# Attention heads by twos with the gates between the pairs, raw float32 weights for the shared expert and the router, and three leading experts with 16 blocks fetched before the sort

## The chip, the cores and the metric

The kernel runs on one core of one Trainium2 chip. The metric is the device time of one execution in microseconds (us); the engines of the core are TensorE (PE, with its weight loads PEld), VectorE (DVE), ScalarE (ACT), GpSimd (POOL) and SyncE (SP), whose queue issues the weight loads here.

## What is computed

Two blocks run one after the other on 256 tokens of 1024 float32 values. Cut to what matters:

```python
# block 1: h = rmsnorm(x); proj = h @ w_in, split into
qa, ka, va, qb, kb, vb, ga, gb = jnp.split(proj, IN_SPLIT_POINTS, axis=-1)
ya = neighbourhood_attention(qa, ka, va, rpb)         # 8 heads of 64, biased and masked scores
qh, kh = axial_rope(rmsnorm(qb, gq)), axial_rope(rmsnorm(kb, gk))
yb = gqa_attention(qh, kh, vb)                        # 8 heads of 64 on 2 key heads
x = x + (sigmoid(ga) * (ya @ w_proj_a) + sigmoid(gb) * (yb @ w_proj_b)) @ w_out
x = x + peer(rmsnorm(x), ...)
# block 2: a token mixer, then the expert layer
scores = sigmoid(xt @ w_router)                       # 64 experts, 8 chosen for each token
routed = sum of gate * (silu(x @ w_gate) * (x @ w_up)) @ w_down over the chosen experts
shared = (silu(xt @ ws_gate) * (xt @ ws_up)) @ ws_down
out = rmsnorm(h + g2 * (routed + shared))
```

## The kernel before, in words

**Weights.** Blocks of 128 x 1024 float32 values (512 KB) come from HBM through SP's queue into rotating buffers. Most products are made from two parts: `split` (L65) lets ACT copy a block to `whi` in the engine's reduced float format and DVE (or POOL, if it is named) subtract to get `wlo`; `mm3` (L78 to L82) then makes three matmuls, high by high, high by low and low by high. A product in plain float32 is one matmul instead, which shows as two records in the trace.

**Block 1** (`block1_mix`). `stationary` (L168) makes one 128-column piece of a projection with the weights in the array, `moving` (L179) makes 512 or 256 columns with the tokens in the array. `qk_block` (L174) makes the q and k of the neighbourhood attention, `moving` its v (`va`), then q (`pq`) and k, v (`pkv`) of the grouped attention. POOL adds the mask to the bias table at once (L246). `attention` (L197) runs one pair of heads: for each head, scores `pS` from its 64 rows (L204), scale and bias on DVE (L211), the maximum (L213, or L216 and L217 without bias), exponentials on ACT (L220), the scaling by the sum (L222, L224), transposes `pT` (L228) and a copy `PT` on ACT (L230); then the value product `pY` with all 128 columns for each head (L235), of which one half of the rows is kept. Between the two attentions stands the rope chain (L268 to L309): squares `sq` (L277), their sums, an inverse root in thirteen small DVE steps (L100 to L110), multiplies by the norms, the rotation (L291 to L299), and the transposes `pqT` (L304) and `pkT` (L308). Sixteen gate blocks `pg` (L316 to L319) stand last in the code; eight of them have their low parts made on POOL; their sigmoids (L321) go four blocks at a time. From here on a list scheduler sets the order on every engine, and it puts the gates' matmuls wherever PE would wait.

**Expert layer** (`moe`). The mixer's output projection, the norm and the shared expert alternate; `gu_block` (L1547) and `shared_up` make the shared expert's first product, L1600 onwards the router. After the router DVE sorts the experts by their number of tokens; `lst` (L1765) holds the sorted list, and SP reads it (L1811) before it can fetch a weight block by rank. The expert of rank r brings six blocks, four `w_gu` and two `w_dn`. The work goes by units of 128 token slots: one rank alone, or 96 + 32, 64 + 64 or four times 32 slots, set by `mixture` (L1445). In one unit's time a PE makes `pgu` (L1559) for it, gathers tokens for later ones (`pga`, L1743), makes the second product `py` (L1578) of the unit before and adds the one before that into the result (`combine`, L1840). The first `STATIC` ranks are units of one rank on tables of their own; as many blocks as fit are fetched before the sort for the experts 0 and onwards. Blocks are used in a fixed order, and each takes the buffer that was used longest ago (`wide_load`, L1407); SP's load waits until PE has used what lay there. The ranks per unit are 1 1 1 2 2 2 4 2 1 2 2 2 1 2 2 4 2 2 2 1 2 2 3 2 2 1, in all 26 units, 50 ranks and 300 blocks, on 25 buffers. Ranks that don't fit run in extra branches (L1940 onwards).

Of the kernel before, what the change touches and what calls it, by code (L numbers as in the profile page):

```python
# [11 lines left out]
F32 = mybir.dt.float32  # L12
# [130 lines left out]
def block1_mix(e, a, x, begin):  # L143
# [22 lines left out]
    qkT = pool.tile([P, 8, T], F32, name="qkT")  # L166

    def stationary(blk, out, eng=None):  # L168
        wh, wl = load_w(e, a["w_in_a"][blk], eng=eng)
# [9 lines left out]
    def moving(blks, width, per):  # L179

        pt = [ps.tile([P, 512], F32, tag="mm", name=uid(e, "pmv"), bufs=e.mm_bufs) for _ in range(2)]
        for i, b in enumerate(blks):
            wh, wl = load_w(e, a["w_in_b"][b])
# [13 lines left out]
    def attention(pair, q_of, k_of, v_of, bias_of, dst):  # L197

        PT = []
        for j in range(2):  # L200
            s = slice(j * 64, (j + 1) * 64)
            pS = ps.tile([P, 2, T], F32, tag="att", name=uid(e, "pS"), bufs=e.att_bufs)
            for i, tt in enumerate((1, 0)):
                nc.tensor.matmul(pS[:, i], q_of(pair)[s, tt * P:(tt + 1) * P], k_of(pair)[s], start=True, stop=True)  # L204
# [41 lines left out]
    nc.gpsimd.tensor_tensor(bias.rearrange("p a b c -> p (a b) c"), bias.rearrange("p a b c -> p (a b) c"),  # L246
                            mask[:, None, :].to_broadcast([P, 48, 64]), op=OP.add)
# [9 lines left out]
    bv = bias.rearrange("p h v c -> p h (v c)")  # L257
    for pair in range(4):
        attention(pair, lambda q: qkT[:, q], lambda q: qkT[:, 4 + q],
                  lambda q, kc: va[:, kc, q * P:(q + 1) * P], lambda h: bv[:, h], yT[0])  # L260

# [18 lines left out]
    for tt, qk in enumerate(qks):  # L280
# [28 lines left out]
        nc.vector.tensor_copy(kT[:, :, tt * P:(tt + 1) * P], p[:, :2])  # L309
    for pair in range(4):  # L310
# [1734 lines left out]
```

## Time and profile before

| what | value |
|---|---|
| time, median of 3 runs | 1756.07 us (1755.73 to 1756.47) |
| profiled execution, its own time | 1763.74 us |
| its span in the trace | 1761.9 us |
| granted TensorE clock over the span | 0.981 |
| PE busy | 1660.2 us (94%) |
| DVE, ACT, POOL busy | 1133.1, 750.5, 190.5 us |
| HBM read | 386.79 MB, 221 GB/s over the span |
| chain that ended last | PE 67%, DVE 18%, DMA 7%, issue 4%, ACT 3% |

The trace is of one execution, whose time is a little over that of the runs; starts and durations are us from the start of its span. An engine's idle time costs something only where the chain runs through it. "Granted clock" is TensorE's clock as a share of full speed.

### The profile page before, as it was taken

What the parts mean: (1) busy time and instruction counts of PE and PEld (TensorE: products, weight loads), DVE (VectorE), ACT (ScalarE), POOL (GpSimd) and SP (SyncE); (2) the same over time, 40 slices, a digit from 0 to 9 for tenths busy, and PEclk for the clock granted to TensorE, in tenths of its full rate; (3) what the DMA queues carried; (4) which work ended last, traced back from release to release, by engine and by line L of the source; (5) the groups of instructions that cost most, each with busy time, mean ns of one, the idle gap of its engine ahead of it and who ended that gap; (6) DMA issues with size and microseconds to landing.
All of it is one profiled execution on the core that took longest, in us unless ns stands there. A gap on an engine that the chain in (4) does not pass through costs nothing.

```text
span 1761.9 us, 29814 instructions
## 1 busy us (share of the span) xinstructions
PE 1660.2 (94%) x11419; PEld 1307.8 (74%) x11419; DVE 1133.1 (64%) x2214; ACT 750.5 (43%) x1224; POOL 190.5 (11%) x95
## 2 busy tenths in 40 slices
PE   6989999899989999999999997987989999999996
PEld 6778888899989999777788776977875444444443
DVE  5675779995989999877777767688673111111112
ACT  3547544444544444444444455655552222222222
POOL 1030001222111222000000003023020000000000
PEclk9999999999999999999999999998999999999999
DMA  6423654556545555587888754532067799999993
GB/s 232 131 84 109 214 163 158 160 158 192 155 126 162 169 171 177 172 283 265 308 283 295 261 165 144 181 118 72 13 238 282 266 392 409 409 402 409 409 409 132
DMA packets 108118, 390.91 MB, mean 222 GB/s; under 512 B 12656, under 2 KB 12944, under 8 KB 107840
## 3 DMA queue, kind: packets, MB, share of 16 engines
q1 hardware_dynamic: 106128, 384.58, 62.7%
q0 software_dynamic: 976, 2.82, 0.5%
q8 instruction: 91, 1.49, 0.3%
q10 hardware_dynamic: 864, 1.53, 0.3%
q14 instruction: 59, 0.48, 0.1%
HBM read 386.79 MB, written 2.10 MB: 221 GB/s over the span
## 4 chain that ended last, share of the span: by engine, by line
PE 67%; DVE 18%; DMA 7%; issue 4%; ACT 3%; POOL 0%; SPq 0%; DVEq 0%; ACTq 0%
PE pgu L1559 11%; PE acc L686 10%; PE py L1578 6%; PE pu L80 5%; PE pu L81 5%; PE pu L82 5%; DVE wlo L67 5%; DMA raw<-in_w_ada 4%; PE pga L1743 3%; PE py L1840 3%; PE pg L632 2%; ACT whi L66 2%; PE pmv L81 1%; PE pmv L82 1%; PE pmv L80 1%
## 5 line engine op out<-in xcount | busy, mean ns | idle before, releaser
L66 ACT ACTIVATE whi<-raw 128x1024 fp32r<-128x1024 f32 x366 | 384.5, 1054 | 307.7 <-PE pu L81 136.7
L67 DVE TENSOR_TENSOR wlo<-raw,whi 128x1024 fp32r<-128x1024 f32 x310 | 383.4, 1239 | 83.1 <-ACT whi L66 82.0
L82 PE MATMUL pu<-pxT,wlo 128*128 128x256 f32 x1024 | 289.7, 283 | 9.2 <-DVE wlo L67 6.7
L80 PE MATMUL pu<-pxT,whi 128*128 128x256 f32 x1024 | 292.3, 285 | 0.8 <-ACT whi L66 0.8
L81 PE MATMUL pu<-pxT,whi 128*128 128x256 f32 x1024 | 288.9, 282 | 0.0
L686 PE MATMUL acc<-whi,hh 128*128 128x512 f32 x1008 | 280.7, 396 | 8.5 <-ACT hh L66 5.8
L686 PEld LDWEIGHTS acc<-whi,hh 128*128 128x128 f32 x1008 | 189.1, 189 | 53.9 <-ACT hh L66 6.8
L67 POOL TENSOR_TENSOR wlo<-raw,whi 128x1024 fp32r<-128x1024 f32 x56 | 149.6, 2675 | 661.9 <-ACT whi L66 607.2
L82 PEld LDWEIGHTS pu<-pxT,wlo 128*128 128x128 f32 x1024 | 195.3, 191 | 11.1 <-DVE wlo L67 8.1
L80 PEld LDWEIGHTS pu<-pxT,whi 128*128 128x128 f32 x1024 | 195.4, 191 | 1.0 <-ACT whi L66 1.0
L81 PEld LDWEIGHTS pu<-pxT,whi 128*128 128x128 f32 x1024 | 195.4, 191 | 0.0
L1559 PE MATMUL pgu<-raw,xg 128*32 128x512 f32 (+2 forms) x1012 | 193.8, 597 | 0.0
L686 PE MATMUL acc<-wlo,hh 128*128 128x512 f32 x504 | 157.5, 393 | 2.8 <-DVE wlo L67 2.8
L66 ACT ACTIVATE hh<-H 128x256 fp32r<-128x256 f32 x126 | 52.6, 417 | 174.6 <-PE acc L686 169.9
L1559 PEld LDWEIGHTS pgu<-raw,xg 128*32 128x32 f32 (+2 forms) x1012 | 55.6, 124 | 92.3 <-issue 82.1
L686 PEld LDWEIGHTS acc<-wlo,hh 128*128 128x128 f32 x504 | 95.0, 189 | 24.3 <-DVE wlo L67 4.2
L67 DVE TENSOR_TENSOR yl<-py,yh 128x512 fp32r<-128x512 f32 x52 | 36.0, 691 | 110.7 <-ACT yh L66 110.6
L1578 PE MATMUL py<-raw,th 128*32 128x512 f32 (+2 forms) x504 | 99.9, 599 | 0.5 <-ACT th L1572 0.5
L1564 DVE SCALAR_TENSOR_TENSOR hh<-hh,sv,pgu 128x256 f32<-128x256 f32 x26 | 12.4, 478 | 124.5 <-ACT hh L1563 124.5
L771 DVE SCALAR_TENSOR_TENSOR ada<-raw,cs,ada 128x1024 f32<-128x1024 f32 x48 | 61.5, 1282 | 40.6 <-DMA raw<-in_w_ada 40.6
L1746 ACT ACTIVATE xg<-pga 128x256 f32<-128x256 f32 x104 | 40.0, 384 | 111.6 <-PE pga L1743 107.6
L1743 PEld LDWEIGHTS pga<-S,hs 128*128 128x128 f32 x416 | 54.5, 188 | 36.8 <-issue 36.1
(567 smaller groups left out, 2919.5 us busy)
## 6 DMA issues: line engine op xcount, KB each, us to landing
raw<-in_w_gu SPq DMA_DIRECT2D x186, 512.0 KB, 9.6
raw<-in_peer_u SPq DMA_DIRECT2D x128, 512.0 KB, 3.6
raw<-in_peer_v SPq DMA_DIRECT2D x128, 512.0 KB, 4.5
raw<-in_w_dn SPq DMA_DIRECT2D x90, 512.0 KB, 10.1
raw<-in_w_ada SPq DMA_DIRECT2D x48, 512.0 KB, 4.8
raw<-in_w_in_a SPq DMA_DIRECT2D x24, 512.0 KB, 3.6
raw<-in_w2a SPq DMA_DIRECT2D x17, 512.0 KB, 4.4
raw<-in_w_out SPq DMA_DIRECT2D x16, 512.0 KB, 3.6
```

The costliest lines, as they stand in the source:

```text
L66: e.nc.scalar.activation(hi, src, AF.Copy)
L67: (eng or e.nc.vector).tensor_sub(lo, src, hi.bitcast(F32))
L80: nc.tensor.matmul(out, lh, rh, start=first, stop=False)
L81: nc.tensor.matmul(out, lh, rl, start=False, stop=False)
L82: nc.tensor.matmul(out, ll, rh, start=False, stop=last)
L686: nc.tensor.matmul(acc[tt][n], h[l][:, s], w[r][:, n * 512:(n + 1) * 512], start=j == order[0] and i == 0, stop=j == order[-1] and i == 2)
L771: nc.vector.scalar_tensor_tensor(mod[n], w, cs[:, c:c + 1], mod[n], op0=OP.mult, op1=OP.add)
L1559: nc.tensor.matmul(pg[t], xx[:, c, t], ws[i][:, k * 512:(k + 1) * 512], start=c == 0, stop=c == NC8 - 1)
L1578: nc.tensor.matmul(py[q][t], th[:, k, t], w[i][:, q * 512:(q + 1) * 512], start=k == 0, stop=last and k == 1)
L1743: nc.tensor.matmul(p[:, :n].rearrange("p u n -> p (u n)"), hs[i][:, tt, q * P:(q + 1) * P], S[:, tt, :n].rearrange("p u n -> p (u n)"), st ...
L1746: nc.scalar.activation(xg[:, q, :n], p[:, :n], AF.Copy)
L1840: nc.tensor.matmul(acc[tt][n], St[:, tt * P:(tt + 1) * P], y[:, n * 512:(n + 1) * 512], start=first and v == 0 and w == 0, stop=v == len(u ...
```

## The change

1. Block 1 loads its weights with `wide_load` and four instead of two pairs of split buffers.
2. `attention` makes the scores of both heads of a pair in turns, and the value product as 64-column halves of one tile, followed by one split of 128 rows instead of two of 64.
3. The mask add becomes four DVE operations of 768 columns, each ahead of the pair that reads it.
4. The projections `pq`, `pkv` and the rope chain come before the neighbourhood attention; each of the eight pairs is followed by two gate blocks; all splits of the gates are on DVE.
5. The shared expert's first product and the router use raw float32 weights and tokens: 16 matmuls instead of 48 and 8 instead of 24.
6. `STATIC` is 3 instead of 2, so 16 instead of 10 blocks are fetched before SP reads the list. `WIDE` and `MID` give other slot widths to the ranks. There are 25 units with the ranks 1 1 1 1 2 2 4 2 2 2 2 2 2 1 4 2 2 2 2 2 2 4 2 2 1, again 50 ranks and 300 blocks, on 27 buffers.

```diff
     qkT = pool.tile([P, 8, T], F32, name="qkT")
+    load = wide_load(e, [(e.stage, e.raw_bufs)], [(e.stage, e.w_bufs), (pool, 2)])
...
+        heads = [slice(j * 64, (j + 1) * 64) for j in range(2)]
+        pSs = [ps.tile([P, 2, T], F32, tag="att", name=uid(e, "pS"), bufs=e.att_bufs) for _ in heads]
+        for i, tt in enumerate((1, 0)):
+            for s, pS in zip(heads, pSs):
+                nc.tensor.matmul(pS[:, i], q_of(pair)[s, tt * P:(tt + 1) * P], k_of(pair)[s], start=True, stop=True)
         PT = []
-        for j in range(2):
-            s = slice(j * 64, (j + 1) * 64)
-            pS = ps.tile([P, 2, T], F32, tag="att", name=uid(e, "pS"), bufs=e.att_bufs)
-            for i, tt in enumerate((1, 0)):
-                nc.tensor.matmul(pS[:, i], q_of(pair)[s, tt * P:(tt + 1) * P], k_of(pair)[s], start=True, stop=True)
+        for j, pS in enumerate(pSs):
...
-        pY = ps.tile([P, 2, T], F32, tag="att", name=uid(e, "pY"), bufs=e.att_bufs)
-        for j in range(2):
-            for kc in range(2):
-                nc.tensor.matmul(pY[:, j], v_of(pair, kc), PT[j][:, kc], start=kc == 0, stop=kc == 1)
-        for j in range(2):
-            s = slice(j * 64, (j + 1) * 64)
-            split(e, dst[0][s, pair], dst[1][s, pair], pY[s, j])
+        pY = ps.tile([P, 512], F32, tag="mm", name=uid(e, "pY"), bufs=e.mm_bufs)[:, :T]
+        for kc in range(2):
+            for s, pt in zip(heads, PT):
+                nc.tensor.matmul(pY[s], v_of(pair, kc)[:, s], pt[:, kc], start=kc == 0, stop=kc == 1)
+        split(e, dst[0][:, pair], dst[1][:, pair], pY)
...
-    nc.gpsimd.tensor_tensor(bias.rearrange("p a b c -> p (a b) c"), bias.rearrange("p a b c -> p (a b) c"),
-                            mask[:, None, :].to_broadcast([P, 48, 64]), op=OP.add)
...
+    def gate(b):
+        p = ps.tile([P, 512], F32, tag="mm", name=uid(e, "pg"), bufs=e.mm_bufs)
+        stationary(8 + b, p[:, :T])
+        nc.scalar.activation(sg[:, b], p[:, :T], AF.Copy)
...
+    def masked(h):
+        if h % 2 == 0:
+            v = bias[:, h:h + 2].rearrange("p a b c -> p (a b) c")
+            nc.vector.tensor_tensor(v, v, mask[:, None, :].to_broadcast([P, 12, 64]), op=OP.add)
+        return bv[:, h]
...
+    for pair in range(4):
+        attention(pair, lambda q: qkT[:, q], lambda q: qkT[:, 4 + q],
+                  lambda q, kc: va[:, kc, q * P:(q + 1) * P], masked, yT[0])
+        for b in (2 * pair, 2 * pair + 1):
+            gate(b)
     for pair in range(4):
         attention(pair, lambda q: qT[:, q], lambda q: kT[:, q // 2],
                   lambda q, kc: vb[:, kc, q // 2].rearrange("p a b -> p (a b)"), None, yT[1])
-
-
-    sg = keep.tile([P, 16, T], F32, name="sg")
-    for b in range(16):
-        p = ps.tile([P, 512], F32, tag="mm", name=uid(e, "pg"), bufs=e.mm_bufs)
-        stationary(8 + b, p[:, :T], nc.gpsimd if b < 8 else None)
-        nc.scalar.activation(sg[:, b], p[:, :T], AF.Copy)
+        for b in (8 + 2 * pair, 9 + 2 * pair):
+            gate(b)
...
-STATIC = 2
-WIDE = 7
-MID = 16
+STATIC = 3
+WIDE = 6
+MID = 14
...
-RAW0 = 4
-RAW1 = 3
+RAW0 = 12
+RAW1 = 5
...
-    def gu_block(pg, xh, xl, b, w):
+    def gu_block(pg, x, b, w):
         for k in range(2):
             c = 2 * b + k
-            s = slice(k * 512, (k + 1) * 512)
-            for j, (l, r) in enumerate(((xh, 0), (xh, 1), (xl, 0))):
-                nc.tensor.matmul(pg, l[:, c], w[r][:, s], start=c == 0 and j == 0, stop=c == NC8 - 1 and j == 2)
+            nc.tensor.matmul(pg, x[:, c], w[:, k * 512:(k + 1) * 512], start=c == 0, stop=c == NC8 - 1)
...
-        mm3(e, p[:, :T], wh[:, c], wl[:, c], hT[0][:, c], hT[1][:, c], c == 0, c == NC8 - 1)
+        nc.tensor.matmul(p[:, :T], wr[:, c], hT[:, c], start=c == 0, stop=c == NC8 - 1)
```

The order that comes of it, at three places. PE, before, at the rope chain: `pqT` and `pkT` are the transposes of the rotated q and k, `pg` are gates.

```order
L82 MATMUL pg_1208<-hT_97,wlo_1212 128x256
L80 MATMUL pg_1208<-hT_97,whi_1211 128x256
L304 MATMUL pqT_884<-ident,qk_841 128x128 x4
L308 MATMUL pkT_890<-ident,kd_880 128x128 x2
L81 MATMUL pg_1208<-hT_98,whi_1211 128x256
L82 MATMUL pg_1208<-hT_97,wlo_1212 128x256
L80 MATMUL pg_1240<-hT_97,whi_1243 128x256
```

PE, after the change, at the same chain; `pmv` is the last projection of k and v, `pS_711` to `pS_826` are the scores of the first two pairs.

```order
L82 MATMUL pmv_572<-whi_605,hT_98 128x256
L205 MATMUL pS_711<-qkT 128x256
L205 MATMUL pS_712<-qkT 128x256
L205 MATMUL pS_711<-qkT 128x256
L205 MATMUL pS_712<-qkT 128x256
L205 MATMUL pS_825<-qkT 128x256 x2
L205 MATMUL pS_826<-qkT 128x256 x2
L298 MATMUL pqT_679<-ident,qk_636 128x128 x4
L302 MATMUL pkT_685<-ident,kd_675 128x128 x2
L298 MATMUL pqT_700<-ident,qk_644 128x128 x4
```

Where gates stood on both sides of the transposes, now only four score products stand between the last projection and the first transpose; the first gate comes after both halves of q and the first pair's probabilities.

ACT, after the change, between the gates of the second pair and the third pair (`sg` are gates, `S_945` and `S_964` the third pair's two heads, `PT` the copy of the transposed probabilities).

```order
L310 ACTIVATE sg<-pg_875 128x256
L66 ACTIVATE whi_1138<-raw_1136 128x1024
L310 ACTIVATE sg<-pg_907 128x256
L331 ACT_TABLE_LOAD
L331 ACTIVATE sg<-sg 128x1024
L223 ACT_TABLE_LOAD
L223 ACTIVATE S_945,sm_947<-S_945,mx_946 128x256 x2
L223 ACTIVATE S_964,sm_966<-S_964,mx_965 128x256 x2
L233 ACTIVATE PT_962<-pT_957 128x512
```

The sigmoid of the first four gates and its two table loads stand between the last of these gates and the third pair's exponentials; before, other gates' copies stood on either side of such a sigmoid.

SP, before, ahead of its first read of the sorted list (`raw` and `ada` are buffers).

```order
L1417 DMA raw_14343<-in_w_gu 128x1024
L1417 DMA raw_14345<-in_w_dn 128x1024
L1417 DMA ada_9413<-in_w_dn 128x1024
L1811 TENSOR_LOAD lst
L1811 ISA x2
```

And after the change:

```order
L1427 DMA raw_14258<-in_w_gu 128x1024
L1427 DMA raw_14260<-in_w_dn 128x1024
L1427 DMA raw_14262<-in_w_dn 128x1024
L1427 DMA raw_14264<-in_w_gu 128x1024
L1427 DMA raw_14266<-in_w_gu 128x1024
L1427 DMA raw_14268<-in_w_gu 128x1024
L1427 DMA raw_14270<-in_w_gu 128x1024
L1427 DMA ada_9400<-in_w_dn 128x1024 x2
L1824 TENSOR_LOAD lst
```

Six more blocks, those of the third leading expert, stand ahead of the read.

## Rows read from the trace of the kernel before

**Rows 1.** Windows: start:end, length, busy of PE, PEld, DVE, ACT, POOL (records), PE clock, DMA share, GB/s

```profile
14.20:54.50 40.30, 36.85 (x243) 34.21 (x242) 22.60 (x22) 12.26 (x12) 6.78 (x1) 0.96 0.58 188
54.50:173.10 118.60, 109.67 (x686) 93.28 (x686) 78.68 (x159) 71.03 (x150) 19.66 (x8) 0.97 0.32 98
...
1430.00:1728.00 298.00, 297.84 (x1997) 132.59 (x1994) 47.81 (x106) 64.18 (x150) 0.00 (x0) 1.00 1.02 408
...
110.00:120.00 10.00, 6.81 (x46) 6.67 (x46) 8.69 (x15) 5.00 (x6) 3.08 (x2) 0.83 0.31 93
```

**Rows 2.** Timeline of POOL and DVE, block 1's start: start, length, engine, line, operation

```profile
16.90 6.78 POOL L246 TENSOR_TENSOR bias<-bias,mask 128x3072 f32<-128x3072 f32 x1 [15.58 <-DMA mask<-in_na_mask]
...
19.38 5.38 DVE L67 TENSOR_TENSOR wlo<-raw,whi 128x1024 fp32r<-128x1024 f32 x1 [0.55 <-ACT whi L66]
```

**Rows 3.** DVE's groups from 44 to 180 us: total busy, mean ns of one

```profile
L67 DVE TENSOR_TENSOR wlo<-raw,whi 128x1024 fp32r<-128x1024 f32 x20 | 24.5, 1224 | 16.8 <-ACT whi L66 16.6
```

**Rows 4.** PE's waits from 14 to 215 us: total us, times, longest

```profile
PE pqT L304 <- DVE qk L299: 4.1, 2, 2.9
PE pqk L82 <- DVE wlo L67: 3.5, 1, 3.5
```

**Rows 5.** Timeline of PE, gate matmuls after the first wait for the rotated q

```profile
113.72 0.41 PE L80 MATMUL pg<-hT,whi 128*128 128x256 f32 x1
113.94 0.41 PE L81 MATMUL pg<-hT,whi 128*128 128x256 f32 x1
...
115.06 0.28 PE L81 MATMUL pg<-hT,whi 128*128 128x256 f32 x1
115.18 0.28 PE L82 MATMUL pg<-hT,wlo 128*128 128x256 f32 x1
```

**Rows 6.** Timeline of PE, scores of two heads, of one head, and value products

```profile
54.43 1.14 PE L204 MATMUL pS<-qkT 64*128 64x256 f32 x8
...
62.44 1.89 PE L235 MATMUL pY<-PT,va 128*128 128x256 f32 x8
...
129.24 1.13 PE L204 MATMUL pS<-kT,qT 64*128 64x256 f32 x4
```

**Rows 7.** The chain that ended last, expert layer: start, length, engine, line, records

```profile
1323.13 5.81 PE pgu L1552 x24
...
1348.27 3.43 PE pgu L1559 x8
...
1380.27 1.88 PE py L1840 x8
...
1385.59 3.57 PE pgu L1559 x32
...
1708.42 1.88 PE py L1840 x8
```

**Rows 8.** Timeline of DVE, the rope chain's first squares and first sum

```profile
90.66 0.81 DVE L277 TENSOR_TENSOR sq<-qk 128x640 f32<-128x640 f32 x1
...
92.72 2.00 DVE L277 TENSOR_TENSOR sq<-qk 128x640 f32<-128x640 f32 x1
...
111.16 0.68 DVE L299 TENSOR_TENSOR qk<-qk,ro 128x512 f32<-128x512 f32 x1
```

**Rows 9.** ACT's groups from 44 to 180 us: total busy, mean ns of one

```profile
L230 ACT ACTIVATE PT<-pT 128x512 f32<-128x512 f32 x16 | 9.5, 600 | 10.0 <-PE pT L228 9.9
...
L220 ACT ACTIVATE S<-pS,mx 128x256 f32<-128x256 f32 x16 | 7.4, 470 | 3.1 <-DVE mx L217 3.1
...
L321 ACT ACTIVATE sg<-sg 128x1024 f32<-128x1024 f32 x4 | 4.2, 1060 | 0.1
...
L321 ACT ACT_TABLE_LOAD x3 | 3.8, 1283 | 0.1
```

**Rows 10.** Windows in the expert phase, columns as in rows 1

```profile
1380.00:1390.00 10.00, 10.00 (x61) 4.67 (x63) 2.53 (x5) 2.48 (x6) 0.00 (x0) 1.00 0.59 179
...
1728.00:1732.00 4.00, 4.00 (x12) 1.82 (x11) 0.28 (x1) 0.38 (x1) 0.00 (x0) 1.00 0.33 131
```

More of the change, by code (lines that the diff above doesn't have):

```diff
@@ L182, in moving @@
         for i, b in enumerate(blks):
-            wh, wl = load_w(e, a["w_in_b"][b])
+            wh, wl = load(a["w_in_b"][b])
             wh, wl = (w.rearrange("p (c n) -> p c n", c=per) for w in (wh, wl))
@@ L1445, in mixture @@
 def mixture():
-    few = iter(range(LIGHT, REST))
+    few = list(range(LIGHT, REST))
+    n = MID - WIDE
     kinds = [[shared((r, P)) for r in range(STATIC, WIDE)],
-             [shared((r, 96), (next(few), 32)) for r in range(WIDE, MID)],
-             [shared((r, 64), (r + 1, 64)) for r in range(MID, LIGHT, 2)]]
-    few = list(few)
-    kinds.append([shared(*((r, 32) for r in few[i:i + 4])) for i in (0, 4)] + [shared((few[8], 32), (few[9], 32), (few[10], 64))])
+             [shared((WIDE + i, 96), (few[i], 32)) for i in range(n)],
+             [shared((r, 64), (r + 1, 64)) for r in range(MID, LIGHT, 2)],
+             [shared(*((r, 32) for r in few[i:i + 4])) for i in range(n, len(few), 4)]]
     at = lambda k, j, n: j / (n - 1) if k == 0 else (j + 0.5) / n
@@ L1474, in moe @@
     mod = m.mod
-    load = wide_load(e, [(early, RAW0), (e.stage, e.raw_bufs)], [(early, 4), (e.stage, e.w_bufs)])
+    load = wide_load(e, [(early, RAW0), (e.stage, e.raw_bufs)], [])
     def add_to(t, p, n, g):
@@ L1503, in moe @@
     square(0, 0)
-    wg = [load(a["ws_gu"][b]) for b in range(2)]
+    wg = [load(a["ws_gu"][b], True) for b in range(2)]
     for i in range(4):
@@ L1512, in moe @@
     add_to(1, po[1], 0, mod[2])
-    wg.append(load(a["ws_gu"][2]))
-    wr = load(a["w_router"], eng=nc.gpsimd)
+    wg.append(load(a["ws_gu"][2], True))
+    wr = load(a["w_router"], True)
     square(1, 0)
@@ L1522, in moe @@
     hs = [pool.tile([P, 2, D], F32R, name=f"hs{i}") for i in range(2)]
-    hT = pool.tile([P, 2, NC8, T], F32R, tag="ehT", name="ehT")
-    hT = [hT[:, i] for i in range(2)]
+    hT = pool.tile([P, NC8, T], F32, tag="ehT", name="ehT")
     load.raw.extend([(pool, RAW1, "raw")] * RAW1)
@@ L1528, in moe, with turn_in @@
         normed(0, r, n)
-    lows = [turned(e, h[0], 4 * n, 0, *hT) for n in range(2)]
+    def turn_in(tt, n):
+        p = ps.tile([P, 4, P], F32, tag="tr", name=uid(e, "ptr"), bufs=e.tr_bufs)
+        for k in range(4):
+            nc.tensor.transpose(p[:, k], h[tt][:, (4 * n + k) * P:(4 * n + k + 1) * P], e.ident)
+        nc.scalar.activation(hT[:, 4 * n:4 * n + 4, tt * P:(tt + 1) * P], p, AF.Copy)
+    for n in range(2):
+        turn_in(0, n)
     add_to(1, m.po[1], 1, mod[2])
     square(1, 1)
-    for f in lows:
-        f()
     r = root(1)
@@ L1593, in moe @@
         normed(1, r, n)
-    wg.append(load(a["ws_gu"][3], eng=nc.gpsimd))
-    lows = [turned(e, h[1], 4 * n, 1, *hT) for n in range(2)]
-    for f in lows:
-        f()
+    wg.append(load(a["ws_gu"][3], True))
+    for n in range(2):
+        turn_in(1, n)
     load.raw.extend([(mod[k], None, None) for k in (2, 4)])
@@ L1620, in moe @@
     wd = [load(a["ws_dn"][k], True) for k in range(2)]
+    used = len(wg) + 1 + len(wd)
+    mine = [q for q in load.raw if q[0] is early]
+    load.raw[:] = (mine[used:] + [q for q in load.raw if q[0] is not early]
+                   + [(e.stage, e.w_bufs, t) for _ in range(e.w_bufs) for t in ("whi", "wlo")] + mine[:used])
     units = [[(r, 0, P, 0)] for r in range(STATIC)] + mixture()
@@ L1626, in moe @@
         pre.append(load((a["w_gu"], a["w_dn"])[which][(4, 2)[which] * r + b], True))
-    load.raw[:0] = [(early, 4, t) for _ in range(4) for t in ("whi", "wlo")]
-    load.raw[:0] = [(e.stage, e.w_bufs, t) for _ in range(e.w_bufs) for t in ("whi", "wlo")]
     hsh, psh = [], []
@@ L1943, in moe @@
             with tc.If(v[2] > 0):
-                run([shared((r, 64), (r + 1, 64), base=64) for r in range(MID, LIGHT, 2)] + [shared((MID, P), base=P)])
+                run([shared((r, 64), (r + 1, 64), base=64) for r in range(MID, LIGHT, 2)]
+                    + [shared((r, 64), (r + 1, 64), base=P) for r in (MID, MID + 2)])
             with tc.If(v[1] > 0):
                 run([shared((r, P), base=96) for r in range(WIDE, MID)]
-                    + [shared(*((r, 32) for r in range(WIDE, WIDE + 4)), base=224)])
+                    + [shared(*((r, 32) for r in range(q, q + 4)), base=224) for q in (WIDE, WIDE + 4)])
             with tc.If(v[0] > 0):
```

16 lines of the change are left out of this document (7 added, 9 removed).

## The prediction

> **What bounds the kernel now.** I read the page's shares first, then the execution cut into windows, the engine waits of block 1, the timelines around them, and for the expert phase the chain that ended last, SP's order of loads and the DMA rate. The profiled execution took 1763.74 us (span 1761.9), 7.67 us over the median of the runs, 1756.07. Every term below is a difference within that execution, and I carry the sum to the median. TensorE is the bound nearly everywhere, for different reasons in the stretches that the diff touches. In block 1, between the end of the va projection (54.5) and the end of the sixteen gate blocks (173.1), it is busy 109.67 of 118.60 us at a granted clock of 0.97 [rows 1]: the scheduler fills nearly every wait with gate matmuls. In the expert phase it is busy 297.84 of 298.00 us, and the DMA engines are full in the same stretch at 408 GB/s [rows 1]. Two limits lie on each other there, and this decides the largest term.
>
> The printed order shows the same rows on every engine between the end of the gates and the start of the expert layer, so I let that middle stretch (173 to 1276 us) shift as a whole.
>
> **Block 1, the start (14 to 54 us).** POOL's mask add takes 6.78 us and a VectorE split beside it 5.38 us [rows 2], where the splits of block 1 average 1.22 [rows 3]. PE waits 3.5 us for that split [rows 4]. The change takes the POOL operation away and puts four mask adds on VectorE, each of 768 columns; by the split's 1.22 us for 1024 [rows 3] I estimate 0.9 us each, in a stretch where VectorE is little over half busy (22.60 of 40.30 us [rows 1]). So 3.5 us of wait go, and about 1.5 us of slow clock behind it: after another wait, matmuls of the same shape start 0.21 us apart, then 0.12 [rows 5]. **Minus 5.0**: the va projection ends near 49.5. If VectorE's adds land in front of a needed split it is minus 3.
>
> **Block 1, from va to the end of the gates.** I walk the new order on PE, with old durations.
>
> *Work.* Scores: two heads back to back are 8 records in 1.14 us, one head alone 4 records in 1.13 [rows 6], so the two row halves already run together where they meet. Before they meet in two pairs only; now in all eight, 1.1 us a pair instead of 2.2. The value product, 1.89 us for 8 records [rows 6], becomes two 64-column halves. No row has two such halves at once; the bounds are 0.95 (together) and 1.89 (one after the other). I take 0.95, since the expert units run four 32-column tiles in the time of one full one: 32 records in 3.57 us against 8 in 3.43 [rows 7]. The gates keep their 384 matmuls at 0.1195 us, 2.87 us a block.
>
> *The rope hole.* pq and pkv (10.9 + 5.75 us) now come first and end at 66.2; two pairs of scores fill PE to 68.4. Then it needs the rotated q, and the order has no gate between. Before, the same chain on VectorE went from the first square at 90.66 to the first sum's end at 111.84, 21.2 us [rows 8], while PE had gates to do. In it operations were stretched by POOL's splits running beside them, as the second square, 2.00 us instead of 0.81 [rows 8]; there are no such splits now. I count the new VectorE order with undisturbed durations: squares and their sums 3.0, pair 0's softmax pieces and one split 5.2, thirteen small steps 2.6, six long multiplies and rotations 6.2, together 17. So the first transposes of q stand at 83.5: **15 us of empty PE**, where before its waits on this chain were 4.1 us [rows 4]. Second half of q, its transposes, pair 0's probabilities: the gates start near 90.
>
> *The pairs.* Each is followed by two gate blocks, 5.74 us. Pairs 1, 3 and 6 have their softmax finished beneath the gates: they cost transposes, one 0.60 us copy [rows 9] and products, 2.7 us each. Pairs 2, 4 and 7 do not: the second half of their scores stands behind the gates, and for 2 and 4 ScalarE first does the gate's copy (0.4, by the exponential's 0.47 for as many columns), a table load (1.28), the sigmoid of four gates (1.06) and another table load (1.28) before the exponentials [rows 9]. From the last gate: 4.0, exponentials of two heads 1.9, scale 0.6, transposes 0.5, copy 0.6, products 0.7: 8.3 us, plus 1.5 of slow clock. Pair 7 goes without the sigmoid but with a table load, 7.7 plus 1.5; pair 5 is 6.5 plus 1. Together 90 + 8 × 5.74 + 2.1 for pair 0's slow clock and refill + 3 × 2.7 + 2 × 9.8 + 9.2 + 7.5, less some 1 us of gate matmuls that slip in: 181.5. Before it was 173.1: **plus 8.4** net of the 5.0 gained. The ends are plus 4 (holes shorter, the clock stays up) and plus 14 (the 64-column halves in turn, 0.95 × 8 = 7.6, less what falls in holes).
>
> A rule speaks against this arrangement. The rows show that after a wait of 2.9 us [rows 4] the matmuls came 0.21 us apart, and 0.12 later [rows 5]: in 110 to 120 us the granted clock was 0.83 [rows 1], part of the window at 1.2 GHz and part at 2.4. The Trainium skill, TensorE: Matmul & The Clock Gate, section What's actually happening, says that TensorE drops to half its clock when it goes idle and must be busy for some time before it gets it back; this trace agrees. By the rule alone each of my six holes is followed by a cold stretch, and by the rows too, so the sum stays; a longer cold stretch is rival 2.
>
> **MoE front.** Raw float32 weights remove five ScalarE, three VectorE and two POOL splits. PE's own work grows: a float32 512-column matmul takes 0.86 us (4 in 3.43 [rows 7]), the three passes 0.24 × 3 = 0.73 (24 in 5.81 [rows 7]). Sixteen such steps and eight router steps (0.43 for 0.36) add 2.7 us. The VectorE chain to the router loses some 4 us. PE is full for most of it: **minus 2**, between 0 and minus 4.
>
> **Expert phase.** PE's pace is 15.63 us a unit, from the combine rows at 1380.27 and 1708.42 with 21 units between [rows 7], whether a unit holds one rank (6 blocks) or four (24). One unit fewer is minus 15.6 if the blocks are there. A 512 KB block at 408 GB/s takes 1.285 us, so a two-rank unit takes 15.4 us of transfer, a four-rank unit 30.8. The lead must come from single units, and while those run the buffers are full and the queue stands: 179 GB/s in 1380 to 1390 [rows 10]. By the time k blocks are used, k plus the buffers can be fetched. Before: 25 buffers, three leading singles of 18 blocks, used by 1348.27 + 46.9 = 1395.2; the other 257 blocks take 330, to 1725. The trace ends its stream at about 1729.3 (131 of 409 GB/s in 1728 to 1732 [rows 10]), so this count is 4 early. After: 27 buffers, **four** leading singles, 24 blocks used by 1346.3 + 62.5 = 1408.8; the 16 prefetched blocks only fill the buffers sooner. The four-rank unit at place 22 of 25 needs blocks up to 270: 219 more, 281 us, so 1690, with the 4 us 1694. Unstopped, PE would want them 5.5 us before its end at 1346.3 + 22 × 15.63 = 1690.2, at 1684.7. PE then waits 5 to 9 us there; before, by the same count, the place of block 270 had 11 us in hand. So **minus 6 to minus 10, taken as minus 7.5** (15.6 less 8.1). The ends: minus 15.6 with no stall, minus 2 if the transfers lose another 5 us.
>
> The overflow branches are not taken in either: with the drawn inputs the longest list at each rank fits its slots (107 of 128 from rank 3, 89 of 96 from 6, 60 of 64 from 14, 31 of 32 from 30).
>
> **Sum:** 8.4 − 2 − 7.5 = −1.1, so 1755.0 us against 1756.07. The bound of no change is 0.2%, 3.5 us, about what a measurement of this kernel can tell from nothing.
>
> **Rivals.**
>
> *1, faster.* The lead holds (SP keeps its buffers fuller than my count, which takes a whole unit's blocks as freed only at its end) and the holes of block 1 are a few us shorter. For it: no PE wait on a weight block over 0.8 us anywhere before. Against: the full rate, 408 GB/s over 298 us [rows 1]. Minus 14 and minus 2 with plus 7: about −9, 1747.
>
> *2, slower.* The clock. If after each of the six holes not 1.5 us are lost but most of the two gate blocks that follow run at 1.2 GHz (48 × 0.09 = 4.3 us), block 1 loses another 13 to 17 and the unit saved does not repay it: −1.1 + 14 = +13; half of that, +6, about 1763. It decides from 2.3 us lost per hole. For it: PE's share between holes is 5.74 us of work to 8 of waiting. Against: before, three cold stretches ended within 1.7 to 3.4 us.
>
> *3, slower as well.* The unit count does less than it says: the stream stands longer in the four singles, and PE ends on it, minus 2 instead of minus 7.5: +4.5, 1760.5.
>
> **How the numbers follow.** My forecast 0.38, its own range 1750 to 1760 (faster 0.12, same 0.23, slower 0.03); rival 1 0.27 (faster 0.24, same 0.03); rival 2 0.20 (slower 0.17, same 0.03); rival 3 0.15 (slower 0.11, same 0.04). Together faster 0.36, same 0.33, slower 0.31. The range leaves a tenth on either side: 1745 to 1766.
>
> **What would show it.** Right: the va projection ends near 49.5; PE empty for about 15 us before the first transpose of q; five holes of 4 to 6 us after gates, with the granted clock near 0.85 in their windows; gates end near 181; the expert units 15.6 us apart until one of four ranks late in the run waits 5 to 9 us on w_gu or w_dn. Wrong: gates ending before 175 or after 190; no wait on weights at all (rival 1), or waits in several units (rival 3).

## The result, and the profile after the change

The changed kernel takes 1777.91 us (median of 4 runs, 1773.41 to 1781.12), where the kernel before takes 1755.9: a ratio of 1.0126, 95% interval 1.0099 to 1.0153. It is 22 us slower; the forecast was 1755.0 with a range to 1766, so it was wrong in size and in sign.

The profiled execution of the change took 1773.41 us, its fastest, and that of before 1763.74, 7.8 us over its median. The two spans therefore differ by 9.7 us only (1771.6 and 1761.9), and the places are compared stretch by stretch. First the windows of the changed kernel, with the columns of [rows 1], over the start of block 1, the stretch that held the gates before, and the expert phase:

```profile
14.20:54.50 40.30, 40.30 (x263) 37.45 (x262) 26.76 (x32) 15.45 (x16) 0.00 (x0) 1.00 0.67 220
54.50:173.10 118.60, 93.41 (x553) 72.48 (x552) 63.16 (x141) 57.62 (x122) 0.00 (x0) 0.83 0.27 80
...
1430.00:1728.00 298.00, 295.39 (x1986) 127.40 (x1984) 44.82 (x100) 60.41 (x144) 0.00 (x0) 1.00 1.02 405
```

The start went as forecast: PE is never idle, at full clock. In the second stretch PE's busy time fell from 109.67 to 93.41 us and its granted clock from 0.97 to 0.83. PE's waits in block 1, the view of [rows 4], name the reasons:

```profile
PE pqT L298 <- DVE qk L293: 9.6, 2, 7.7
PE pT L231 <- DVE S L227: 7.3, 2, 4.5
PE pS L205 <- ACT S L223: 5.4, 1, 5.4
PE pS L205 <- DVE S L214: 4.0, 3, 2.7
PE pS L205 <- DVE wlo L67: 2.2, 1, 2.2
```

Where pieces that both kernels contain start or end, the delay against before grows and shrinks like this (starts, from the groups by tile of both traces; the last row is the end):

| piece | before | after | later by |
|---|---|---|---|
| last gate matmul of block 1 | 173.0 | 194.0 | 21.0 |
| first `pu` of the `peer` experts | 281.3 | 300.7 | 19.4 |
| last `acc` of them | 1082.1 | 1099.9 | 17.8 |
| first output projection of the expert layer | 1282.3 | 1293.2 | 10.9 |
| first routed unit | 1348.1 | 1356.1 | 8.0 |
| end of the span | 1761.9 | 1771.6 | 9.7 |

Block 1 carries the loss. (Single executions of three runs below ran at a granted clock of 0.56 to 0.83 over the whole span and are left out, two of four in the run with `pY` on the gates' ring in the kernel before, for which the other two are given without a ratio.) Between 700 and 1290 us, where both kernels run the same code, the delay falls from 19.4 to 10.9 us, and that is a difference of the two executions and not of the kernels: the last row but two of the table, the same place of the same code, stood at 1279.3, 1281.3, 1282.3 and 1285.7 in four executions with block 1 as before. In all traces of this case the way from the first `pu` to that place takes between 992 and 1003 us. The other stretches repeat far better, so below they are compared one by one as well. The expert layer's front gained 2.9 us in this pair of traces, and the routed units with one unit less lost 1.7.

The last part of the chain that ended last shows what became of that unit:

```profile
1637.90 1.87 PE py L1853 x8
...
1650.10 10.07 DMA raw<-in_w_gu
1660.28 10.77 DMA raw<-in_w_dn
1671.17 10.08 DMA raw<-in_w_gu
1681.36 10.12 DMA ada<-in_w_gu
...
1695.18 1.97 PE py L1853 x8
...
1702.57 10.10 DMA raw<-in_w_dn
1712.79 10.12 DMA raw<-in_w_gu
...
1731.04 1.92 PE py L1853 x8
```

Five units lie between the combines (`py` L1853) at 1637.90 and 1731.04; at 15.63 us they would take 78.2, and they take 93.1. The chain runs through six loads there, and the units take 15 us longer than PE's pace. PE's busy time hides this (295.39 of 298.00 us above), since the wait falls on its weight loads:

```profile
PEld pgu L1571 <- DMA raw<-in_w_gu: 11.1, 13, 1.2
PEld py L1590 <- DMA raw<-in_w_dn: 3.8, 5, 1.1
```

And the stream, in windows, was full to its end at 1741.2 (119 of 409 GB/s in the last four):

```profile
1728.00:1740.00 12.00, 12.00 (x66) 5.39 (x66) 1.86 (x3) 2.30 (x6) 0.00 (x0) 1.00 1.02 407
1740.00:1744.00 4.00, 4.00 (x13) 2.04 (x12) 0.00 (x0) 0.53 (x2) 0.00 (x0) 1.00 0.30 119
```

### The profile page after: what moved, and what is told of

It is laid out like the page before. It is cut to its first block, busy times and chain, and to the rows that moved or that the text cites. A ratio compares the mean times of both kernels' runs of the same rounds, so it can differ in the third digit from the quotient of the medians.

```text
span 1771.6 us, 29526 instructions
## 1 busy us (share of the span) xinstructions
PE 1658.2 (94%) x11301; PEld 1291.6 (73%) x11301; DVE 1113.4 (63%) x2204; ACT 742.3 (42%) x1209; POOL 162.1 (9%) x84
## 4 chain that ended last, share of the span: by engine, by line
PE 65%; DVE 16%; DMA 10%; issue 3%; ACT 3%; POOL 0%; DVEq 0%; SPq 0%; ACTq 0%
PE acc L696 9%; PE pgu L1571 9%; DMA raw<-in_w_ada 5%; PE pu L80 5%; PE pu L81 5%; PE pu L82 5%; PE py L1590 5%; DVE wlo L67 4%; PE pga L1756 3%; PE py L1853 2%; DMA raw<-in_w_gu 2%; PE pg L642 2%; ACT whi L66 1%; DMA raw<-in_w_dn 1%; PE pmv L82 1%
## 5 line engine op out<-in xcount | busy, mean ns | idle before, releaser
L66 ACT ACTIVATE whi<-raw 128x1024 fp32r<-128x1024 f32 x361 | 379.6, 1054 | 312.6 <-PE pu L81 138.2
L82 PEld LDWEIGHTS pu<-pxT,wlo 128*128 128x128 f32 x1024 | 194.0, 189 | 14.0 <-DVE wlo L67 10.8
L80 PEld LDWEIGHTS pu<-pxT,whi 128*128 128x128 f32 x1024 | 194.0, 190 | 0.9 <-ACT whi L66 0.9
L81 PEld LDWEIGHTS pu<-pxT,whi 128*128 128x128 f32 x1024 | 194.1, 190 | 0.0
L1571 PE MATMUL pgu<-raw,xg 128*32 128x512 f32 (+2 forms) x980 | 187.8, 597 | 1.7 <-DMA raw<-in_w_gu 1.6
L67 POOL TENSOR_TENSOR wlo<-raw,whi 128x1024 fp32r<-128x1024 f32 x46 | 128.0, 2786 | 498.1 <-ACT whi L66 496.7
L66 ACT ACTIVATE hh<-H 128x256 fp32r<-128x256 f32 x126 | 52.6, 417 | 173.0 <-PE acc L696 166.7
L1759 ACT ACTIVATE xg<-pga 128x256 f32<-128x256 f32 (+1 forms) x104 | 39.0, 375 | 116.5 <-PE pga L1756 112.3
```

Of the source, the lines that this page charges most:

```text
L66: e.nc.scalar.activation(hi, src, AF.Copy)
L67: (eng or e.nc.vector).tensor_sub(lo, src, hi.bitcast(F32))
L80: nc.tensor.matmul(out, lh, rh, start=first, stop=False)
L81: nc.tensor.matmul(out, lh, rl, start=False, stop=False)
L82: nc.tensor.matmul(out, ll, rh, start=False, stop=last)
L1571: nc.tensor.matmul(pg[t], xx[:, c, t], ws[i][:, k * 512:(k + 1) * 512], start=c == 0, stop=c == NC8 - 1)
```

## The experiments

Two theories came from this comparison. **A:** in block 1 the scheduler could not bring gates forward, because the value product `pY` of each pair now takes its PSUM tile from the ring of four banks that the gates use; a ring gives its banks out in the order of the code, so a gate can't stand ahead of a `pY` that comes before it in the code. **E:** in the expert phase the weight stream is the bound, and four leading single units make it stand longer than three. Against A: the code order itself (C), heads by twos in themselves (D). Against E: the wait is only an echo of block 1 (F).

### Block 1 alone

Edit: the function `block1_mix` of after in the kernel before.

> Block 1 as changed, the expert layer as before. In the traces of the two kernels the gates of block 1 end 21.0 us later after the change (194.1 instead of 173.1). Theory A (block 1 alone carries the loss, the expert layer gives about nothing): 1776 to 1780 us, gates' end at 193 to 195, and block 1's PE clock near 0.83 between 54 and 173 us. Rival B (a good part of the 21 us is taken up again by the middle stretch, and the loss comes from the expert layer): 1757 to 1766 us.

Measured: 1782.03 us where before took 1759.67, ratio 1.0118 (1.0089 to 1.0148); last gate at 193.1, clock 0.83 in the second stretch. Theory A's range is met by the ratio (the median lies 2 us above it, and the kernel before stood 4 us higher in these rounds too), rival B falls: block 1 alone loses what the whole change loses.

### One line of it undone

```diff
-        pY = ps.tile([P, 512], F32, tag="mm", name=uid(e, "pY"), bufs=e.mm_bufs)[:, :T]
+        pY = ps.tile([P, 2, T], F32, tag="att", name=uid(e, "pY"), bufs=e.att_bufs)[:, 0]
```

> As the run with only block 1 changed, with one edit: the value product pY takes its PSUM bank from the ring of the scores, as before the change, and no longer from the ring of the gates. Theory A: the scheduler could not bring gates forward because each pair's pY stood ahead of them in the gates' ring; with pY elsewhere gates fill the rope chain again, PE's waits before 173 us fall from 29 to under 8 us, gates end near 158 to 165, time 1741 to 1749 us. Rival C (the code order, q and the rope chain ahead of the first pair, is itself the cause): gates end after 185, time over 1768. Rival D (the interleaved heads and the 64-column value products are slow in themselves): between, near 1757 to 1765.

Measured: 1750.26, ratio 0.9946 (0.9928 to 0.9964). That one line turns +20.8 us into −9.5. The printed PE order of this kernel has five gate blocks where the changed one has none, between the first scores and the first transposes of q:

```
L205 MATMUL pS_712<-qkT 128x256
L80 MATMUL pg_761<-hT_97,whi_764 128x256
...
L81 MATMUL pg_989<-hT_98,whi_992 128x256
L298 MATMUL pqT_679<-ident,qk_636 128x128 x4
```

and PE's waits in block 1 are down to these:

```profile
PE pT L231 <- DVE S L227: 2.3, 1, 2.3
PE pqT L298 <- DVE qk L293: 1.7, 2, 1.2
PE pY L238 <- ACT PT L233: 0.9, 2, 0.5
PE pp L80 <- ACT whi L66: 0.8, 1, 0.8
PE ptr L126 <- DVE ph L456: 0.6, 1, 0.6
```

Rival C falls as the cause of the loss, since the code order is the same here, and rival D with it, since the heads go by twos here as well and the kernel is faster than before. The gates' last matmul is at 151.1, earlier than the 158 to 165 expected, since the gates are used up before the last pairs, which then stand among the projections that follow. The median was 1 us above the range that I gave for it.

### The same line put into the kernel before

```diff
-        pY = ps.tile([P, 2, T], F32, tag="att", name=uid(e, "pY"), bufs=e.att_bufs)
+        pY = ps.tile([P, 2, T], F32, tag="mm", name=uid(e, "pY"), bufs=e.mm_bufs)
```

> The kernel before with one edit: the tile of the value product pY comes from the ring of four PSUM banks of the projections and gates, instead of the ring of the scores. Theory A (the place of pY in the gates' ring keeps the scheduler from bringing gates forward): the printed order then has no gate before the last pair, PE waits out the rope chain (about 15 us) and the softmax of four pairs (about 4 us each), and the time rises by 25 to 40 us over the kernel before. Rival H (the ring is not the cause; the order of the code is): within 5 us of the kernel before.

Measured: 1783.31 and 1783.73, 25 us over before's 1758.34, at the lower end of theory A's range; H falls. In its trace the first gate matmul stands at 146.7 us, beside the value product of the last pair, where the kernel before has it at 89.1: no gate has passed the `pY` of a pair that comes before it in the code. Its waits show the emptied rope chain (4.1 us before, [rows 4]), with nothing else changed:

```profile
PE pqT L304 <- DVE qk L299: 14.7, 2, 12.9
PE pT L228 <- DVE S L224: 4.2, 6, 1.6
```

### Heads one after the other again

Edit: block 1 as changed, with `attention` of before.

> Block 1 as changed but with the attention function of before (heads one after the other, a 128-column value product on the scores' ring, two splits for a pair); the expert layer as before. Against the run with pY on the scores' ring this shows what heads by twos and 64-column products are worth alone. Theory A with the interleaving worth its work (scores 6 us, value product 2.6 us by 1.56 instead of 1.89 for 8 pairs, where PE is full): 6 to 10 us slower than that run, that is about 4 us below to 3 us above the kernel before. Rival D (heads by twos gain nothing where gates fill): within 2 us of that run.

Measured: 1741.24, ratio 0.9892 (0.9838 to 0.9946); below both expectations. Heads by twos, with their 64-column products and single split, are not a gain in this code order but a loss: the first `pu` matmul stands at 265.5 with the old heads and at 271.2 with the pairs. Two more traces with this block 1 and the pairs (below) have 270.8 and 270.2, one more with the old heads 267.8, so the loss is 2 to 6 us. The ratios alone wouldn't show it, as their intervals overlap.

```profile
L80 PE MATMUL pu<-pxT,whi x1024: 277/280/415, 265.5 to 688.7; 128*128 128x256 f32 x171
...
L80 PE MATMUL pu<-pxT,whi x1024: 277/280/415, 271.2 to 690.7; 128*128 128x256 f32 x171
```

A pair by twos holds both tiles of the scores' ring, so the next scores wait for both heads; the old heads pass them on singly. From 145 to 190 us, where the last pairs stand after the gates, PE is busy 40.95 of 45.00 us with the pairs and 43.91 with the old heads. That the two tiles are the reason is argued, not tested.

### The code order of before, gates last

Edit: block 1 as changed, but the neighbourhood pairs ahead of `pq`, the gates after all pairs, and `pY` on the scores' ring.

> Block 1 as changed but in the code order of before (neighbourhood pairs ahead of the projections of q, k and v of the grouped attention, gates last) and with pY on the scores' ring; expert layer as before. Against the run with pY on the scores' ring it shows what the code order is worth. If the gain over the kernel before comes from the mask and the gates' splits leaving POOL, this run is as fast as that one, 7 to 11 us below the kernel before. If the order (the rope chain ahead of the pairs, so that gates fill it and the pairs later) gives it: within 4 us of the kernel before.

Measured: 1738.47, ratio 0.9884 (0.9853 to 0.9916), 20 us under before: neither expectation. So the order of the change costs about 12 us against the old order, by twos and with `pY` out of the way (first `pu` at 271.2 and 259.3). Here PE is full through all of block 1, as its windows say:

```profile
14.20:54.50 40.30, 40.30 (x267) 37.01 (x266) 28.46 (x36) 16.39 (x19) 0.00 (x0) 1.00 0.67 223
54.50:173.10 118.60, 118.47 (x825) 100.44 (x824) 82.17 (x167) 76.74 (x152) 0.00 (x0) 1.00 0.38 117
```

The first `pu` is at 259.3, where the kernel before has it at 281.3. Of these 22 us, 12 are PE's idle time in the two windows of before ([rows 1]), which is gone; the rest is less work on PE and its clock. Which part of the change removes how much (the mask and the splits away from POOL, the wider weight buffers, scores by twos, one split for a pair) no run separates. The old heads, which were faster in the other order, weren't tried in this one.

### One sigmoid instead of four

```diff
-    for b in (0, 8, 4, 12):
-        nc.scalar.activation(sg[:, b:b + 4], sg[:, b:b + 4], AF.Sigmoid)
+    nc.scalar.activation(sg, sg, AF.Sigmoid)
```

> As the run with only block 1 changed (pY on the gates' ring), with one edit: one sigmoid over all sixteen gates behind the last of them, instead of four over four gates each. It measures the table loads and sigmoids that stand in two of the holes. If the holes are as long as ScalarE's chain before the exponentials makes them: 3.6 us off each of two holes, some slow clock with it, and up to 4 us back behind the gates, 4 to 9 us faster than that run. If other work of the holes (scores on VectorE, transposes at the low clock) is as long: within 2 us of it.

Measured: 1772.58, ratio 1.0076 (1.0048 to 1.0103), against 1.0118 with four: 0.42%, 7 us, which is in the expected range but not clear of noise, as the two intervals overlap. The traces show where the edit acts. The last gate matmul stands at 186.6 us instead of 192.8, so the table loads and sigmoids did lengthen two holes, by about what was expected. But most of it is paid back behind the gates, where the single sigmoid takes ScalarE 3.62 us:

```profile
189.69 3.62 ACT L330 ACTIVATE sg<-sg 128x4096 f32<-128x4096 f32 x1
```

So the first `pu` stands at 298.4 instead of 299.1. The other 7 us of difference between the two traces arise after 1101 us, in code that both share. By the traces block 1 gains about 1 us by this edit, less than either the range or the ratio says, and that the time came out as expected is luck.

### The expert layer alone

Edit: `block1_mix` of before in the kernel after.

> Block 1 as before, the expert layer as changed. Theory E (the weight stream is the bound: with four single units in front it stands longer, and PE waits out the unit saved at the four-rank unit at place 22): the first unit 2 to 4 us earlier than in the kernel before, the stream ends 385 us after the first unit's start, PE's end 0 to 4 us earlier, time 1752 to 1756. Rival F (the wait seen in the changed kernel came from the shift of block 1 and not from the unit list): the whole unit is gained, 1736 to 1742.

Measured: 1760.16 against 1759.67, ratio 0.9999 (0.9985 to 1.0012). Theory E stands and F falls. From the first unit to the span's end it takes 415.5 us (1350.2 to 1765.7), as long as in the changed kernel, and 413.8 before, with one unit less. The waits stand at the same two units, with the combines 26.0 and 20.5 us apart.

### The single units later

```diff
-    at = lambda k, j, n: j / (n - 1) if k == 0 else (j + 0.5) / n
+    at = lambda k, j, n: (j + 1) / n if k == 0 else (j + 0.5) / n
```

> As the run with only the expert layer changed, with one edit: the three single units of the list stand at 1/3, 2/3 and the end of it instead of the start, the middle and the end, so three singles lead instead of four and the first four-rank unit has place 6. Theory E: the stream ends near 377 us after the first unit's start instead of 385, no wait of PE on a weight block over 1 us, 25 units at 15.6 us: 1738 to 1742. Rival G (any list of 25 units is bound by the stream at 409 GB/s, whatever its order): 1750 to 1756, with the wait at another four-rank unit.

Measured: 1753.92, ratio 0.9965 (0.9948 to 0.9982), 6 us faster than before. The stream ended where E put it, 377.5 us after the first unit (1342.2 to 1719.7, by the last window). Yet PE still waited: the chain goes through two loads between the combines at 1672.91 and 1708.73, two units that take 35.8 us instead of 31.3, 4.5 too many.

```profile
1672.91 1.97 PE py L1843 x8
1680.26 10.10 DMA raw<-in_w_dn
1690.48 10.11 DMA raw<-in_w_gu
1708.73 1.92 PE py L1843 x8
...
1718.00:1722.00 4.00, 4.00 (x12) 1.99 (x11) 0.04 (x1) 0.77 (x2) 0.00 (x0) 1.00 0.42 170
```

The time and the remaining wait are those of rival G, at the fast end of its range, and not E's: I expected no wait, and some 16 us more. What G denied, that the order matters, is shown all the same: the same list with its singles elsewhere is 6 us slower (0.9999, with an interval clear of this one), and from the first unit to the end it takes 415.5 us against 407.0 here.

### Two leading units instead of three

```diff
-STATIC = 3
+STATIC = 2
```

> As the run with only the expert layer changed and its single units late, and STATIC at 2: two leading singles with 10 blocks fetched before the sort, the third expert a unit of the list, 25 units as before. Theory E (the stream's idle time in the leading singles sets PE's end; blocks fetched early only fill the buffers sooner): the stream ends near 369 us after the first unit's start, no wait on weights over 1 us, 4 to 8 us faster than with three leading singles, 10 to 14 us faster than the kernel before. Rival I (the 16 blocks fetched before the sort are worth something): slower than with three.

Measured: 1748.55, ratio 0.9938 (0.9910 to 0.9966), 10 us faster than before and 5 faster than with three leading singles, though only 10 blocks are fetched before the sort. The two ratios' intervals overlap, but the traces settle it. From the first unit to the end it takes 401.1 us (1345.8 to 1746.9), and 401.3 to 402.2 in three more kernels with this list (below), against 407.0 with three leading singles. Before it took 413.8, in all seven traces with the old list to within 0.2. In the first 64 us of the units the stream runs at 365 GB/s here, at 292 with three leading singles and at 252 with four, as theory E has it, and it ends 371 us after the first unit (369 expected). Late combines are evenly spaced, where the last four-rank units stand, so no unit waits for its weights and rival G falls for good:

```profile
1660.14 1.88 PE py L1843 x8
1675.99 1.98 PE py L1843 x8
1691.23 1.92 PE py L1843 x8
1706.43 1.92 PE py L1843 x8
```

So the six more blocks fetched early, which the change is named after, are worth nothing here (rival I falls), and the single unit that comes with them costs the stream 5 to 6 us.

### The parts together

The changed kernel with only the `pY` line undone:

> The changed kernel with one line undone: pY on the scores' ring. Theory A: the 29 us that this line costs in block 1 come back and the expert layer gives about nothing: 7 to 11 us faster than the kernel before, 1747 to 1752 where that takes 1758.

Measured: 1750.22, ratio 0.9947 (0.9929 to 0.9965). With single units late and two leading units as well:

> The changed kernel with three edits: pY on the scores' ring, single units late, STATIC 2. If the two parts add up: about 9 us from block 1 and 10 to 14 us from the expert layer, so 19 to 23 us faster than the kernel before. If block 1's gain moves the expert phase against another limit: under 14 us.

Measured: 1740.75, ratio 0.9867 (0.9810 to 0.9925): 17.6 us by the medians, 23 by the ratio. With the old heads in place of the `pY` line:

> The changed kernel with three edits: the attention function of before (heads one after the other, the value product on the scores' ring), single units late, STATIC 2. In the traces block 1 gains 15.8 us with the old heads (first matmul of the experts' u at 265.5 instead of 281.3) and the expert layer about 12 us. If they add up: 1728 to 1733 us where the kernel before takes 1756 to 1760, 25 to 30 us faster. If the stream of weights is by now the bound wherever block 1 ends: 10 to 14 us.

Measured: 1735.18, ratio 0.9858 (0.9834 to 0.9882): 23 us by the medians, 25 by the ratio, at the low end of the 25 to 30. With the code order of before and `pY` on the scores' ring:

> Block 1 of the run with the gates last and pY on the scores' ring (20 us under the kernel before), expert layer with two leading singles and the single units late (10 us under it). If the two parts add: 1726 to 1731 us where the kernel before takes 1758. If the stretch between takes up what block 1 gains, or the weight stream does: 1734 to 1740, no faster than either part's best so far.

Measured: 1726.06, ratio 0.9804 (0.9771 to 0.9837): 33.7 us faster than the kernel before, 52 faster than the change. So the parts add up (20 and 10 us, and more).

In the traces they add up in all three. Against the kernel before, the first `pu` is 11.1, 13.5 and 22.7 us earlier, and from the first unit to the end it takes 11.6, 12.3 and 12.5 us less: 22.7, 25.8 and 35.2 together, near the 23, 25 and 34 us of the ratios. What the medians of the first two fall short by lies within what executions differ by between 700 and 1290 us.

## Why the prediction was wrong, point by point

Two terms of the sum failed, the pairs of block 1 by 12.6 us and the expert phase by 9.2. They make up nearly all of the 23 us between the forecast (minus 1.1) and the result (plus 22).

**The start of block 1** was right: PE has no idle time there, q, k and v end at 66.5 us (66.2 forecast).

**The rope hole** was right in its place and its end: the first transposes of q stood at 81.73 (83.5 forecast), the first gates at 89.6 (90). It isn't the 15 us of empty PE, though. PE idles for 10.9 us, as the second pair's scores, which the forecast had done by 68.4, wait for the tiles of the first pair's and run until 74.0, in part at the low clock. The order was read correctly as one without gates there. What I did not ask was why the scheduler had put none, and so the cause, one line of the diff, stayed unnamed: `pY` on the gates' ring. The walk carried that cause's cost along without knowing it, so the miss lies elsewhere.

**The pairs** are the step that failed, by 12.6 us: gates' end at 194.1 instead of 181.5. Gate by gate from the trace: pairs 1, 3 and 6 took 3.44 us each (2.7 forecast), pair 2 11.8 and pair 4 12.1 (9.8), pair 7 9.8 (9.2), and pair 5 13.4 (7.5). The value products of pair 1 on PE, the copies and weight loads in front of them, and pair 2's hole on PE:

```profile
97.93 1.07 ACT L233 ACTIVATE PT<-pT 128x512 f32<-128x512 f32 x2
98.57 1.56 PE L238 MATMUL pY<-PT,va 128*64 128x256 f32 x8 [0.28 <-ACT PT L233]
98.57 0.19 PEld L238 LDWEIGHTS pY<-PT,va 128*64 128x64 f32 x2 [0.68 <-ACT PT L233]
99.06 0.62 PEld L238 LDWEIGHTS pY<-PT,va 128*64 128x64 f32 x6 [0.29 <-ACT PT L233]
...
106.00 0.70 PE L205 MATMUL pS<-qkT 64*128 64x256 f32 x4
107.55 2.53 PE L205 MATMUL pS<-qkT 64*128 64x256 f32 x8 [0.84 <-DVE S L214]
112.82 2.07 PE L231 MATMUL pT<-ident,S 128*128 128x128 f32 x8 [2.74 <-DVE S L227]
114.82 1.12 PE L238 MATMUL pY<-PT,va 128*64 128x256 f32 x2
```

Three things were mis-sized. First, the value product: 8 records take 1.56 us at full clock, not 0.95 (the bounds were 0.95 and 1.89), 0.6 us a pair, nearly all of what pairs 1, 3 and 6 have over. The 64-column halves do run together, as I took them to, where both are ready. But the forecast counted one copy of the probabilities on ScalarE and there are two, one for each head, which end 0.5 us apart. The first head's first product runs alone from 98.57, while the second head's weight loads wait until 99.06 for the second copy, and so the last product has no partner either; only the two in between run side by side. Before, with both products of one head ahead of the other head's, the first head's could run beneath the second copy ([rows 6]: 1.89 without a break). Second, the low clock: I priced it as 1.5 us of slow gates behind a hole, but it fell on the hole's own matmuls, 2.53 us for scores of 1.14, 2.07 for transposes of 1.03. The slow scores cost nothing here, as PE still waits 2.74 us for VectorE behind them; the transposes and the value product behind that wait do. The windows of pairs 2 and 4 and of the gates behind them:

```profile
106.00:118.00 12.00, 8.29 (x34) 4.80 (x34) 7.41 (x18) 8.41 (x16) 0.00 (x0) 0.72 0.29 87
118.00:123.00 5.00, 5.00 (x44) 5.00 (x43) 3.77 (x9) 3.55 (x11) 0.00 (x0) 1.00 0.01 3
132.40:145.00 12.60, 7.24 (x30) 4.21 (x29) 4.13 (x11) 8.25 (x16) 0.00 (x0) 0.73 0.28 83
145.00:150.00 5.00, 5.00 (x44) 5.00 (x44) 1.65 (x2) 1.54 (x3) 0.00 (x0) 1.00 0.02 5
```

The gates run at 2.4 GHz throughout (1.00), the hole in front of them at 1.2 for more than half of its time (0.72 and 0.73). So rival 2 was right that the clock makes the holes longer, and wrong about where. Third, pair 5: the order gave both heads of pair 6 their scores and exponentials inside pair 5's hole, with a split of 1.22 us on VectorE between, and I had counted pair 5's own work only. The value product and the clock had their place in the range's upper end (+14); the six us of pair 5 had none.

**The front of the expert layer** was right within its range of 0 to 4 (2 forecast): 2.9 us less between the first output projection and the first unit in the two traces. Over all traces this stretch takes 64.1 or 65.8 us with the old expert layer and 62.9 to 64.6 with the new one, so like against like it is nearer to 1.2.

**The expert phase** was wrong by 9 us (minus 7.5 forecast, plus 1.7 seen), with the stream right: by the forecast's count it ends some 386 us after the first unit, and it ended after 385.1. The step that failed is the one that placed PE's need. It asked only for the last block of the four-rank unit at place 22 and let PE catch it at that unit's end. But its 16 first blocks are wanted at its front, so PE lost 10.3 us there (combines at 1669.11 and 1695.04, 25.9 apart instead of 15.6), and its eight last blocks, which its second product wants two units later, cost another 5 (1710.37 to 1730.88, 20.5 apart); the two-rank units behind, 15.4 us of transfer for 15.63 of work, rebuild no lead. Rival 3 (the unit yields nothing because PE ends on the stream) is what happened; it had 0.15.

**The sum** put plus 8.4 against minus 9.5. Measured, block 1 alone is plus 20.8 (1.0118) and the expert layer alone minus 0.2 (0.9999): together, within their intervals, what the whole change shows, plus 22.

## What to carry to other kernels

A scheduler fills a wait only with work whose tiles it may allocate. When a tile moves to another ring of PSUM banks, ask which later work takes its banks from that ring: it can no longer pass. Where the printed order shows a hole that was filled before, look for the edit that closed it before pricing the hole; here one line stood between a loss of 22 us and a gain of 9, and three small edits more (the code order of the pairs, one formula, one constant) brought the gain to 34.

A unit of work that costs the same whatever it holds is only saved if the stream keeps up. Count the stream's idle time at the start, where buffers are full, and put the units that use few blocks where that doesn't happen. And look for such waits at the weight loads and in the spacing of the units: PE's busy share doesn't show them.

Where two matmuls are to run in two halves of the array, ask when the operands of each are ready: they only pair up if both are.

## What the runs showed of the hardware that was not expected

Scores of two heads in the two row halves of the array overlap almost fully (8 records in 1.14 us, where one head's 4 take 1.13). The expert units' four 32-column tiles do too ([rows 7]: 32 records in 3.57 us against 8 in 3.43). The value products in two 64-column halves look as if they didn't, with 8 records in 1.56 us against 1.89 for full columns one after the other. But of these, the records of the second and third product start within 0.01 us of each other, and the six records from the second product on take 1.08 us:

```profile
89.88 1.08 PE L238 MATMUL pY<-PT,va 128*64 128x256 f32 x6
```

Six records in turn would take 1.4 (an estimate, six eighths of 1.89). So these halves overlap as well, and the 1.56 us come from the order in which their operands arrive. The Trainium skill, TensorE: Matmul & The Clock Gate, Part 3: Packing small matmuls — row/col tiling, says that small matmuls on different row or column tiles of the array run at the same time, and gives 2.38 times for three column tiles. This trace agrees for row halves (1.98 times), for 32 columns and for 64-column halves, each where the operands of both are there.

The granted clock inside a 12 us hole was 0.72, with 1.00 in the 5 us of dense gates right behind it: what a hole costs is paid by the matmuls in it.
